# Loading the operands of RWKV's inverses in two halves, scaling its output later, and loading three attention units first

## The chip, the cores and the metric

The kernel runs on one core of one Trainium2 chip. The metric is device time in microseconds from launch to the last output. Its engines are TensorE (PE; its weight loads are listed apart as PEld), VectorE (DVE), ScalarE (ACT), GpSimd (POOL) and SyncE (SP), which here only issues DMAs. Every engine works through its own instructions in the order in which the program holds them; an instruction that waits holds up all behind it on its engine.

## The reference

One layer over 2048 tokens of width 1024. `x` is normalised and projected by `w_in`; the columns go to two branches whose outputs, 512 wide each, are joined, projected by `w_out` and added to `x`, with a last norm.

```python
def rwkv7_scan(r, decay, k, v, kk, a):       # 8 heads of 64
    def step(S, inp):
        r_t, w_t, k_t, v_t, kk_t, a_t = inp
        sa = jnp.einsum('bhij,bhj->bhi', S, -kk_t)
        S = (S * w_t[:, :, None, :]
             + sa[..., None] * (kk_t * a_t)[:, :, None, :]
             + v_t[..., None] * k_t[:, :, None, :])
        return S, jnp.einsum('bhij,bhj->bhi', S, r_t)
...
    y = (y - mu) * lax.rsqrt(var + GN_EPS) * gn_g + gn_b      # per head
    y = y + jnp.sum(r * k * r_k, axis=-1, keepdims=True) * v
    return y * jax.nn.silu(gate)

def attend(args):                             # blocks of 128 queries, 8 heads
    logits = jnp.einsum('bqhd,bsd->bqhs', qi, k_idx)          # index scores
    score = jnp.einsum('bqh,bqhs->bqs', wi, jax.nn.relu(logits))
    _, idx = lax.top_k(jnp.where(causal[None], score, -jnp.inf), topk)   # 256 keys
    s = jnp.einsum('bqhr,bqkr->bhqk', qa, c_sel)
    p = jax.nn.softmax(jnp.where(valid[:, None], s, -jnp.inf), axis=-1)
    return jnp.einsum('bhqk,bqkr->bqhr', p, c_sel)
```

## The kernel before

Four phases are written one after the other: `phase_as` (projections, and for every block of queries a mask of the 256 chosen keys, all stored in DRAM), `phase_r` (RWKV), `phase_t` (attention) and `phase_w` (the output projection). A scheduler turns them into one order for each engine. It takes the instruction of the best priority that its own timing says is ready; `e.later(n)` makes priorities worse by n steps, so attention (`later(2)`) and the output (`later(3)`) fill what RWKV leaves, and `tc.issue_after(x)` keeps an instruction behind x. Tiles of one tag share a fixed number of buffers (the last argument of `tl`), and a new tile of that tag waits until the old one has been read.

RWKV is not run token by token. The 2048 tokens are 16 batches n of 128, each of two halves (`chain(..., n, 0)` and `chain(..., n, 1)`) of 64 tokens, and all 8 heads are done at once; two units i = 0, 1 hold four heads each. A batch goes through these steps:

- `prep(n, i)`: loads `ld` (five quantities in one DMA), forms the scaled keys `BK` and queries `X` on DVE (eight operations, lines 950 to 967), and multiplies them on PE into `E`, which DVE copies under a mask (line 977).
- `systems`: `E` holds triangular blocks of 32 x 32, and `dma` carries them to DRAM (`du`, 4 DMAs) and back as `A`, where each of 32 systems stands in four partitions (the source is read four times).
- `inverse`: POOL inverts all of them at once in 31 iterations of two instructions (`Xtmp`, line 1031, and `Xr`, line 1033). The result goes to DRAM (`dx`) and back as `TT` (4 DMAs).
- `chain`: PE solves with `TT` (line 1068) and updates the state `S` (DVE, line 1096), one half batch after the other.
- `tail_norm` and `tail_out`: the norm of the batch's output `y`. DVE forms sums (`gst`), POOL raises them to -1/2 (line 1112), DVE scales `y` (line 1113); PE transposes `y` (line 1120), ACT writes `yo` (line 1126), POOL adds and multiplies (lines 1128, 1129), and SP stores it (line 1130) with the loads of `gr` (line 1124) beside it.

At step n of the loop the kernel runs `inverse` of batch n+1, the norm of batch n-1 behind it, `prep` of batch n+2, and `chain` of batch n. `A` and `Xr` have one buffer each.

Attention has 64 units, p = 0 to 3 (two heads each) by b = 0 to 15 (blocks of 128 queries); unit (p, b) has b+1 key blocks of 128. For every key block PE forms the scores (lines 1261 and 1262), DVE adds the mask (line 1263), ACT takes the exponential, PE transposes the weights of the two heads (line 1295, two transposes a key block), ACT copies them and PE multiplies with the values (line 1304). `load` fetches a unit's keys, queries, mask and gate one unit ahead. The output projection of a block of 128 tokens has 48 matmuls (lines 1381, 1382 and 1384) and needs both branches' results for it; its weights are loaded once RWKV's memory is free.

Of the kernel before, what the change touches and what calls it, by code (L numbers as in the profile page):

```python
# [7 lines left out]
F32 = mybir.dt.float32  # L8
# [6 lines left out]
OP = mybir.AluOpType  # L15
# [3 lines left out]
T = 2048  # L19
# [867 lines left out]
def phase_r(env):  # L887


    e = NS(env)  # L890
# [4 lines left out]
    W = 2 * C  # L895
# [112 lines left out]
    def systems(us):  # L1008

        du = e.dram([2, 2, NU, 32, 32], F32, nm("du"))  # L1010
        A = tl([128, 32, 32], F32, "A")
        for i, u in enumerate(us):
            for k in range(2):
                ps_ = slice(64 * i + k * 32, 64 * i + k * 32 + 32)
                dma(du[i, k].rearrange("u s t -> s u t"),
                    u.E[ps_, :, :, k * 32:k * 32 + 32].rearrange("s h c t -> s (h c) t"))
        dma(A.rearrange("l s t -> l (s t)"),
            du.rearrange("i k u s t -> (i k u) (s t)")[None].to_broadcast([4, 32, 1024]))
        return A

    def inverse(A):

        dx = e.dram([2, 2, NU, 32, 32], F32, nm("dx"))
        Xr = tl([128, 8, 32], F32, "Xr")
        G.memset(Xr, 0.0)
        for j in range(4):
            G.memset(Xr.rearrange("p i t -> p (i t)")[32 * j:32 * j + 32, j:256:36], 1.0)
        tmp = tl([128, 8, 32], F32, "Xtmp")
        for s in range(31):
            m, w = s // 4 + 1, 31 - s  # L1030
            G.tensor_tensor(tmp[:, :m, :w], Xr[:, :m, s:s + 1].to_broadcast([128, m, w]),  # L1031
                            A[:, s:s + 1, s + 1:].to_broadcast([128, m, w]), op=OP.mult)
            m_ = G.tensor_tensor(Xr[:, :m, s + 1:], Xr[:, :m, s + 1:], tmp[:, :m, :w], op=OP.add)  # L1033
        dma(dx.rearrange("i k u (r j) t -> j (i k u) r t", j=4), Xr)
        TT = tl([128, NU, 32], F32, "TT", 2)
        for i in range(2):
            for k in range(2):
                dma(TT[Q[2 * i + k]], dx[i, k].rearrange("u s t -> s u t"))
        return TT, m_.ins
# [60 lines left out]
    def tail_norm(y):  # L1100

        yv = y.rearrange("t c (h i) -> t (c h) i", h=2)
        st = tl([128, 3, NU], F32, "gst", 2)
        V.tensor_reduce(st[:, 0], yv, axis=AX.X, op=OP.add)
        V.tensor_scalar(st[:, 0], st[:, 0], 1.0 / 64, None, op0=OP.mult)
        bc = lambda a: a[:, :, None].to_broadcast([128, NU, 64])
        V.tensor_tensor(yv, yv, bc(st[:, 0]), op=OP.subtract)
        sq = tl([128, NU, 64], F32, "ysq")
        S.activation(sq, yv, AF.Square)
        V.tensor_reduce(st[:, 1], sq, axis=AX.X, op=OP.add)  # L1110
        V.tensor_scalar(st[:, 1], st[:, 1], 1.0 / 64, 64e-5, op0=OP.mult, op1=OP.add)
        m = G.tensor_tensor(st[:, 2], st[:, 1], e.mhalf[:, :NU], op=OP.pow)  # L1112
        V.tensor_tensor(yv, yv, bc(st[:, 2]), op=OP.mult)
        return m.ins

    def tail_out(us, y):

        pt = pst([128, NC, 2, C], "ch", 1)
        for c in range(NC):
            PE.transpose(pt[:, c].rearrange("p a b -> p (a b)"), y[:, c], ident)  # L1120
        for i, u in enumerate(us):
            yo = tl([128, 2, W], F32, "yo", 2)
            gr = tl([128, 2, W], F32, "gr", 2)
            dma(gr, e.d_gr4.rearrange("p (g i) t -> p g i t", i=2)[:, :, u.i, u.sl])
            for g, p in enumerate(u.ps):
                S.activation(yo[:, g].rearrange("p (a b) -> p a b", a=2), pt[:, 2 * g:2 * g + 2, i], AF.Identity,
                             scale=e.gng[:, p:p + 1], bias=e.gnb[:, p:p + 1])
            G.tensor_tensor(yo, yo, u.bv, op=OP.add)
            G.tensor_tensor(yo, yo, gr, op=OP.mult)  # L1129
            dma(e.d_y.rearrange("p (g i) t -> p g i t", i=2)[:, 0:2, u.i, u.sl], yo)  # L1130
# [28 lines left out]
    for n in range(N):  # L1159
# [3 lines left out]
        with e.later():  # L1163
            if nx:
                nx.TT, first = inverse(nx.A)
            if b0:
                with behind(first):
                    tail_norm(y0)
            if new:
                with behind(state):  # L1170
                    new.us.append(prep(n + 2, 0, new.eC, first))
        y = tl([128, NC, 128], F32, "y", 2)
        state = chain(b.us, b.TT, b.eC, y, n, 0)
        with e.later():
            if nx:
                for u in nx.us:
                    prep2(u)
# [7 lines left out]
                tail_out(b0.us, y0)  # L1185
        y0, b0 = y, b
    with e.later():
        tail_norm(y0)
        tail_out(b0.us, y0)


def phase_t(env):
# [11 lines left out]
        return ps.tile(shape, F32, name=nm(tag), tag=tag, bufs=bufs)  # L1204


    sel0 = tl([4, 256], F32, "sel0").rearrange("p (c a b) -> p c a b", c=2, a=2)
    V.memset(sel0, 1.0)
    G.affine_select(sel0, sel0, pattern=[[2, 2], [1, 2], [0, 64]], base=0, channel_multiplier=-1,
                    compare_op=OP.is_equal, fill=0.0)  # L1210
# [108 lines left out]

    units = [(p, b) for p in range(NP) for b in range(NB)]  # L1320
    last, stores, marks = None, [], {}
    load(*units[0])
    for i, u in enumerate(units + [None]):
        out = []
        ready, stores = stores, []
        if i + 1 < len(units):
            with tc.issue_after(load(*units[i + 1])):
                for x in ready:
                    dma(*x)
# [90 lines left out]
```

## Time and profile before

| | |
|---|---|
| three runs | 2094.41, 2101.48 (median), 2104.39 us |
| the profiled execution | 2104.7 us, span 2102.9 us |
| PE busy | 1803.3 us (86%) |
| PE weight loads busy | 1421.8 us (68%) |
| DVE busy | 1296.7 us (62%) |
| ACT busy | 1019.8 us (48%) |
| POOL busy | 795.3 us (38%) |
| mean granted clock of PE | 0.906 |
| DMA over the span | 126 GB/s |

The span runs from the first instruction to the last. Busy shares are means over phases with different limits: the projections end at about 980 us, RWKV with attention in its gaps follows to about 1760 us, and the rest of attention with the output projection makes the end. Idle time of an engine counts only where something late waits for that engine.

### The profile page before, as it was taken

Reading aid. Unit: us, or ns where it says so; the run is one execution under the profiler, and the core shown is the slowest. Engines: PE = TensorE matmul, PEld = TensorE weight load, DVE = VectorE, ACT = ScalarE, POOL = GpSimd, SP = SyncE. Lnnn points to the kernel's source line nnn. Section 1 sums busy time; section 2 is a strip of 40 time slices with the busy share of each in tenths; the row PEclk is TensorE's granted clock in tenths of the full one; section 3 lists DMA queues with packets and bytes.
Section 4 is the critical chain, followed back from the end, with each engine's and each line's share of the span. In section 5 each row is a group of like instructions: output and inputs, shape, how many; then the busy total and the mean of one; then the engine's idle time right before and its main releaser. Section 6 shows DMA issues by size and latency. Waiting matters only on the chain.

```text
span 2102.9 us, 36153 instructions
## 1 busy us (share of the span) xinstructions
PE 1803.3 (86%) x12906; PEld 1421.8 (68%) x12906; DVE 1296.7 (62%) x3050; ACT 1019.8 (48%) x1966; POOL 795.3 (38%) x1925
## 2 busy tenths in 40 slices
PE   5788998879796988986788988886988889899998
PEld 4666877658575867765566766665766667587776
DVE  5532538979779698986656557564756654644432
ACT  4422494453444744441355555454655567643431
POOL 1110124353544354562445645654546650100000
PEclk9778999989798999998799998798988899999999
DMA  7526334332262434234844355343454324744223
GB/s 248 199 94 200 108 101 135 101 115 85 75 239 63 135 107 136 91 95 125 204 102 105 95 136 147 105 119 98 115 143 131 93 78 108 233 128 128 66 93 112
DMA packets 309038, 262.50 MB, mean 125 GB/s; under 512 B 82544, under 2 KB 258288, under 8 KB 307696
## 3 DMA queue, kind: packets, MB, share of 16 engines
q1 hardware_dynamic: 304464, 248.03, 40.1%
q0 software_dynamic: 4384, 12.06, 1.8%
q8 instruction: 104, 1.70, 0.4%
q14 instruction: 86, 0.70, 0.1%
HBM read 166.37 MB, written 97.85 MB: 126 GB/s over the span
## 4 chain that ended last, share of the span: by engine, by line
PE 23%; POOL 14%; DMA 12%; issue 5%; DVE 4%; SPq 1%; ACT 1%; POOLq 0%; DVEq 0%; ACTq 0%
DMA A<-du 6%; POOL Xr L1033 6%; POOL Xtmp L1031 5%; PE om L1304 3%; PE po L1381 3%; PE po L1382 3%; PE po L1384 3%; PE tr L1295 3%; DMA dx<-Xr 2%; PE s L1261 2%; PE s L1262 1%; DMA TT<-dx 1%; DMA ld<-d_rw 1%; POOL yo L1129 1%; POOL gst L1112 1%
## 5 line engine op out<-in xcount | busy, mean ns | idle before, releaser
L577 PE MATMUL pm<-xh,wh 128*128 128x512 f32 x800 | 330.4, 414 | 20.3 <-DVE t L588 11.8
L578 PE MATMUL pm<-xl,wh 128*128 128x512 f32 x800 | 327.0, 409 | 0.0
L579 PE MATMUL pm<-xh,wl 128*128 128x512 f32 x800 | 326.1, 408 | 0.0
L1263 DVE CUSTOM_DVE_ANT_0 sc<-s,mk 128x512 f32<-128x512 f32 (+3 forms) x320 | 187.9, 607 | 102.8 <-PE s L1262 76.0
L1297 ACT ACTIVATE pt<-tr 128x512 f32<-128x512 f32 (+1 forms) x288 | 157.9, 569 | 160.8 <-PE tr L1295 115.9
L1031 POOL TENSOR_TENSOR Xtmp<-Xr,A 128x60 f32<-128x60 f32 (+24 forms) x496 | 146.9, 296 | 225.8 <-DMA A<-du 181.8
L577 PEld LDWEIGHTS pm<-xh,wh 128*128 128x128 f32 x800 | 158.1, 198 | 61.7 <-DVE t L588 13.7
L1270 ACT ACTIVATE sc<-sc,mx 128x128 f32<-128x128 f32 (+15 forms) x128 | 153.0, 1198 | 63.0 <-DVE mx L1269 62.7
L1295 PE MATMUL tr<-ident,sc 128*128 128x128 f32 x1088 | 180.1, 292 | 3.0 <-ACT pt L1297 2.6
L579 PEld LDWEIGHTS pm<-xh,wl 128*128 128x128 f32 x800 | 157.3, 197 | 36.4
L578 PEld LDWEIGHTS pm<-xl,wh 128*128 128x128 f32 x800 | 158.0, 197 | 35.4
L1304 PE MATMUL om<-pt,vt 128*64 128x128 f32 x2176 | 174.0, 295 | 6.2 <-DVE ga L1287 6.2
L1261 PE MATMUL s<-kt,q 128*128 128x512 f32 (+2 forms) x320 | 144.2, 454 | 35.8 <-DVE mx L1263 32.2
L1033 POOL TENSOR_TENSOR Xr<-Xr,Xtmp 128x60 f32<-128x60 f32 (+24 forms) x496 | 151.3, 305 | 37.4
L1304 PEld LDWEIGHTS om<-pt,vt 128*64 128x64 f32 x2176 | 134.2, 146 | 37.6 <-issue 19.6
L1295 PEld LDWEIGHTS tr<-ident,sc 128*128 128x128 f32 x1088 | 133.5, 149 | 33.9 <-issue 11.4
L317 ACT ACTIVATE mk<-x,st 128x1920 bf16<-128x1920 f16 (+5 forms) x72 | 98.0, 1361 | 103.6 <-POOL st L314 103.6
L249 ACT ACTIVATE rl<-lg,wi 128x512 f32<-128x512 f32 (+3 forms) x152 | 94.0, 631 | 99.6 <-PE lg L247 53.1
L1262 PE MATMUL s<-kt,q 128*128 128x512 f32 (+2 forms) x320 | 123.3, 389 | 8.1 <-DMA q<-d_q 8.0
L320 DVE TENSOR_SCALAR_CACHE_REDUCE mk<-x,st 128x2048 bf16<-128x2048 f16 (+5 forms) x72 | 120.6, 1675 | 1.4
L254 DVE SCALAR_TENSOR_TENSOR xs<-rl,wi,xs 128x512 f32<-128x512 f32 (+3 forms) x108 | 73.5, 681 | 60.9 <-ACT rl L249 60.1
L1387 POOL TENSOR_TENSOR st<-st 128x1 f32<-128x1 f32 x16 | 3.1, 195 | 277.1 <-ACT po L1386 277.1
(329 smaller groups left out, 3937.7 us busy)
## 6 DMA issues: line engine op xcount, KB each, us to landing
wraw<-in_w_in_dram SPq DMA_DIRECT2D x42, 512.0 KB
d_rw<-t SPq DMA_DIRECT2D x80, 256.0 KB
ld<-d_rw SPq DMA_DIRECT2D x32, 640.0 KB
q<-d_q SPq DMA_DIRECT2D x128, 128.0 KB
d_q<-t SPq DMA_DIRECT2D x32, 256.0 KB
d_kt<-t SPq DMA_DIRECT2D x32, 256.0 KB
kt<-d_kt SPq DMA_DIRECT2D x32, 256.0 KB
A<-du SPq DMA_DIRECT2D x16, 512.0 KB
```

Of the source, the lines that this page charges most:

```text
L577: PE.matmul(pm, wh[:, k], XH[g][:, k], start=k == 0, stop=False)
L578: PE.matmul(pm, wh[:, k], XL[g][:, k], start=False, stop=False)
L579: PE.matmul(pm, wl[:, k], XH[g][:, k], start=False, stop=k == KD - 1)
L1031: G.tensor_tensor(tmp[:, :m, :w], Xr[:, :m, s:s + 1].to_broadcast([128, m, w]), A[:, s:s + 1, s + 1:].to_broadcast([128, m, w]), op=OP.mult)
L1033: m_ = G.tensor_tensor(Xr[:, :m, s + 1:], Xr[:, :m, s + 1:], tmp[:, :m, :w], op=OP.add)
L1261: PE.matmul(pS[:, :wp], qh[:, h, qs], k[:, h, :wp], start=True, stop=False)
L1262: PE.matmul(pS[:, :wp], ql[:, h, qs], k[:, h, :wp], start=False, stop=True)
L1263: V.tensor_tensor_reduce(out=rows[h][:, c0:c0 + w], in0=pS[:, :w], in1=mk[:, c0:c0 + w], scale=1.0, scalar=LOW, op0=OP.add, op1=OP.max, ac ...
L1270: marks[p, b] = S.activation(rows[h][:, :n], rows[h][:, :n], AF.Exp, bias=mx[:, h, 4:5], accum_out=sums[:, h:h + 1]).ins
L1295: PE.transpose(pt[:, i, h], rows[h][:, (kb + i) * 128:(kb + i) * 128 + 128], ident)
L1297: S.activation(w[:, :m], pt[:, :m], AF.Copy)
L1304: PE.matmul(po[HALF[h]], v[:, (kb + i) % 4, HALF[h]], w[:, i, h], start=kb + i == 0, stop=kb + i == b)
```

## The change

The operands of the inverses lie in two tiles: `A`, rows 0 to 15 of every system, with two buffers, and `A2`, rows 16 to 31, with one. Each has its own DMA of 256 KB, and `inverse` reads from the one that holds row s. `tail_norm` returns the scaling as a function, and the loop calls it after the first half of `chain`, behind that half's state update, where it used to stand ahead of it; after the loop it is called at once. `yo` has one buffer instead of two. `sel0` no longer has a tile of its own: it uses one of the four score buffers `sc`. The first three units' loads are issued at a priority three steps better, ahead of RWKV's own, and the loop loads from the fourth on.

```diff
     def systems(us):
 
         du = e.dram([2, 2, NU, 32, 32], F32, nm("du"))
-        A = tl([128, 32, 32], F32, "A")
+        A = tl([128, 16, 32], F32, "A", 2), tl([128, 16, 32], F32, "A2")
         for i, u in enumerate(us):
             for k in range(2):
                 ps_ = slice(64 * i + k * 32, 64 * i + k * 32 + 32)
                 dma(du[i, k].rearrange("u s t -> s u t"),
                     u.E[ps_, :, :, k * 32:k * 32 + 32].rearrange("s h c t -> s (h c) t"))
-        dma(A.rearrange("l s t -> l (s t)"),
-            du.rearrange("i k u s t -> (i k u) (s t)")[None].to_broadcast([4, 32, 1024]))
+        rows = du.rearrange("i k u s t -> (i k u) (s t)")
+        for j in range(2):
+            dma(A[j].rearrange("l s t -> l (s t)"), rows[None, :, j * 512:j * 512 + 512].to_broadcast([4, 32, 512]))
         return A
@@
         for s in range(31):
             m, w = s // 4 + 1, 31 - s
+            row = A[0][:, s:s + 1, s + 1:] if s < 16 else A[1][:, s - 16:s - 15, s + 1:]
             G.tensor_tensor(tmp[:, :m, :w], Xr[:, :m, s:s + 1].to_broadcast([128, m, w]),
-                            A[:, s:s + 1, s + 1:].to_broadcast([128, m, w]), op=OP.mult)
+                            row.to_broadcast([128, m, w]), op=OP.mult)
@@
-        m = G.tensor_tensor(st[:, 2], st[:, 1], e.mhalf[:, :NU], op=OP.pow)
-        V.tensor_tensor(yv, yv, bc(st[:, 2]), op=OP.mult)
-        return m.ins
+        rpow(st[:, 2], st[:, 1])
+        return lambda: V.tensor_tensor(yv, yv, bc(st[:, 2]), op=OP.mult)
@@
-            yo = tl([128, 2, W], F32, "yo", 2)
+            yo = tl([128, 2, W], F32, "yo")
@@
             if b0:
                 with behind(first):
-                    tail_norm(y0)
+                    scale = tail_norm(y0)
...
         state = chain(b.us, b.TT, b.eC, y, n, 0)
         with e.later():
+            if b0:
+                with behind(state):
+                    scale()
             if nx:
                 for u in nx.us:
                     prep2(u)
@@
-        tail_norm(y0)
+        tail_norm(y0)()
         tail_out(b0.us, y0)
@@
-    sel0 = tl([4, 256], F32, "sel0").rearrange("p (c a b) -> p c a b", c=2, a=2)
+    sel0 = tl([128, T], F32, "sc", 4)[0:4, 0:256].rearrange("p (c a b) -> p c a b", c=2, a=2)
@@
-    load(*units[0])
+    with e.later(-3):
+        for u in units[:3]:
+            load(*u)
     for i, u in enumerate(units + [None]):
         out = []
         ready, stores = stores, []
-        if i + 1 < len(units):
+        if 3 <= i + 1 < len(units):
```

The scheduler makes new orders from this, and all of RWKV, attention and output stands a little differently. On SP, a step of the loop where the result of one inverse (`dx`, `TT`) and the operands of the next (`du`, `A`) follow each other, before:

```order
L1034 DMA dx_1459_8400<-Xr_1460_8401 4x256x32
L1015 DMA du_1501_8668<-E_1496_8648 32x8x32 x2
L937 DMA ld_1545_8998<-d_rw_63 128x10x128
L1038 DMA TT_1462_8471<-dx_1459_8400 32x8x32 x4
L1017 DMA A_1502_8669<-du_1501_8668 128x1x1024
L1232 DMA q0_2520_14754<-d_q0_66 64x2x256 x2
```

and the same step now:

```order
L1036 DMA dx_1462_8406<-Xr_1463_8407 4x256x32
L1015 DMA du_1504_8674<-E_1499_8654 32x8x32 x2
L1335 DMA d_y_93<-ga_2423_14339 128x128
L1040 DMA TT_1465_8477<-dx_1462_8406 32x8x32 x4
L1019 DMA A_1505_8675<-du_1504_8674 128x1x512
L1019 DMA A2_1506_8676<-du_1504_8674 128x1x512
L937 DMA ld_1549_9006<-d_rw_63 128x10x128
```

Both halves stand where the one load stood, behind `dx` and `TT` of the inverse before; `ld` has moved behind them. On DVE, the scaling of batch 6's `y` (line 1113) and the second `E` of batch 9 (line 977), before:

```order
L964 TENSOR_TENSOR BK_10858<-ld_10848,L_10852 128x4x64
L979 SCALAR_TENSOR_TENSOR ld_10848<-ld_10848,rkc 128x128 x2
L1269 TENSOR_REDUCE mx_15960<-mx_15960 128x1 x2
L977 TENSOR_TENSOR E_10868<-rp_10869,mask_7751 128x512
L977 TENSOR_TENSOR E_10868<-rp_10870,mask_7751 128x512
L1287 TENSOR_TENSOR ga_15756<-ga_15756,om_15974 128x128
L1263 ISA sc_16073,mx_16075<-s_16077,mk_15953 128x512
L1263 ISA mx_16075 128x1
L1263 ISA sc_16074,mx_16075<-s_16081,mk_15953 128x512
L1263 ISA mx_16075 128x1
L1278 RECIPROCAL sums_15961<-sums_15961 128x2
L1113 TENSOR_TENSOR y_10376<-y_10376,gst_10696 128x512
```

and now, where it is line 1115:

```order
L1098 TENSOR_TENSOR S_1345_7771<-ch_10812,SP_10779 64x4x64 x2
L1115 TENSOR_TENSOR y_10391<-y_10391,gst_10714 128x512
L950 SCALAR_TENSOR_TENSOR L_10870<-restart_7748,ld_10866 128x256
L959 TENSOR_TENSOR BK_10876<-ld_10866 128x4x64
L962 TENSOR_SCALAR ka_10878<-ld_10866,kac,oka 128x128 x2
L1321 TENSOR_TENSOR ga_16102<-ga_16102,om_16375 128x128
L1082 TENSOR_TENSOR SP_10930<-S_1345_7771,eC_9893 64x256 x2
L1267 ISA sc_16476,mx_16477<-s_16501,mk_16340 128x512
```

The scaling stood behind `E`; now it follows the state update `S` and comes ahead of the whole preparation, whose `E` stands 22 rows further down. On SP again, the place of the last inverse's result, before:

```order
L1242 DMA mk_3370_17986<-d_mask15_86 128x2048
L1329 DMA d_y_93<-ga_3249_17503 128x128
L1034 DMA dx_2173_13209<-Xr_2174_13210 4x256x32
L1244 DMA ga_3407_18133<-d_ga_62 128x128
L1038 DMA TT_2176_13280<-dx_2173_13209 32x8x32 x4
L1232 DMA q0_3404_18125<-d_q0_66 64x2x256 x2
L1232 DMA q1_3405_18128<-d_q1_67 64x2x256 x2
L1242 DMA mk_3406_18131<-d_mask0_71 128x128
```

and now:

```order
L1246 DMA mk_3646_18981<-d_mask10_81 128x1408
L1036 DMA dx_2189_13241<-Xr_2190_13242 4x256x32
L1040 DMA TT_2192_13312<-dx_2189_13241 32x8x32 x4
L1335 DMA d_y_93<-ga_3535_18579 128x128
L1248 DMA ga_3647_18983<-d_ga_62 128x128
L1335 DMA d_y_93<-ga_3555_18648 128x128
L1248 DMA ga_3673_19083<-d_ga_62 128x128
L1246 DMA mk_3672_19081<-d_mask11_82 128x1536
```

The next mask to be loaded was that of block 0 of the last p; now it is that of its block 11. Attention stands ten to eleven units further on at this point of RWKV.

## Rows read from the trace of the kernel before

**Rows 1.** Stretches: us, busy of PE, PEld, DVE, ACT, POOL, clock, DMA share, GB/s.

```profile
1101.30:1758.80 657.50, 557.60 (x6390) 433.47 (x6389) 385.48 (x1183) 365.80 (x829) 361.00 (x1030) 0.89 0.43 112
1758.80:2103.00 344.20, 323.64 (x2183) 256.59 (x2182) 144.68 (x363) 149.36 (x304) 22.77 (x57) 0.97 0.41 128
```

**Rows 2.** Waits: engine, line, releaser, us in total, times, longest.

```profile
POOL Xtmp L1031 <- DMA A<-du: 181.8, 14, 18.6
...
DVE y L1113 <- POOL gst L1112: 74.0, 11, 15.6
```

**Rows 3.** SP's issues in one step of RWKV: start, us, what.

```profile
1177.88 0.58 SPq L1034 DMA_DIRECT2D dx<-Xr  x1
1182.59 1.81 SPq L1038 DMA_DIRECT2D TT<-dx  x4
...
1186.94 0.57 SPq L1017 DMA_DIRECT2D A<-du  x1
```

**Rows 4.** POOL's timeline: first product of seven of the inverses.

```profile
1152.10 0.24 POOL L1031 TENSOR_TENSOR Xtmp<-Xr,A 128x31 f32<-128x31 f32 x1 [11.86 <-DMA A<-du]
...
1197.78 0.24 POOL L1031 TENSOR_TENSOR Xtmp<-Xr,A 128x31 f32<-128x31 f32 x1 [14.19 <-DMA A<-du]
...
1250.71 0.24 POOL L1031 TENSOR_TENSOR Xtmp<-Xr,A 128x31 f32<-128x31 f32 x1 [16.65 <-DMA A<-du]
...
1426.84 0.24 POOL L1031 TENSOR_TENSOR Xtmp<-Xr,A 128x31 f32<-128x31 f32 x1 [13.11 <-DMA A<-du]
...
1477.18 0.28 POOL L1031 TENSOR_TENSOR Xtmp<-Xr,A 128x31 f32<-128x31 f32 x1 [12.54 <-DMA A<-du]
...
1531.54 0.24 POOL L1031 TENSOR_TENSOR Xtmp<-Xr,A 128x31 f32<-128x31 f32 x1 [17.18 <-DMA A<-du]
...
1705.71 0.24 POOL L1031 TENSOR_TENSOR Xtmp<-Xr,A 128x31 f32<-128x31 f32 x1 [12.69 <-DMA A<-du]
```

**Rows 5.** The chain of waits through one long step: start, us, what.

```profile
1223.79 1.62 POOL gst L1112
...
1232.80 1.28 DVE E L977 x2
...
1237.71 12.94 DMA A<-du
```

**Rows 6.** SP's issue of the last load of `A`.

```profile
1695.69 0.55 SPq L1017 DMA_DIRECT2D A<-du  x1
```

**Rows 7.** Busy time while that load flows.

```profile
1697.00:1704.60 7.60, 7.60 (x72) 5.77 (x70) 6.14 (x18) 7.27 (x15) 0.00 (x0) 1.00 0.27 76
```

**Rows 8.** The chain of waits: a store of 64 KB of attention.

```profile
1585.72 1.94 DMA d_y<-ga
```

**Rows 9.** SP's issues at the start of RWKV.

```profile
981.01 0.58 SPq L937 DMA_DIRECT2D ld<-d_rw  x1
...
997.12 2.53 SPq L1232 DMA_DIRECT2D q<-d_q  x4
...
1055.67 0.57 SPq L1034 DMA_DIRECT2D dx<-Xr  x1
...
1066.39 1.81 SPq L1038 DMA_DIRECT2D TT<-dx  x4
```

**Rows 10.** Attention's transposes up to 1758.8 us and behind it: count, busy, mean ns.

```profile
L1295 PE MATMUL tr<-ident,sc 128*128 128x128 f32 x758 | 130.0, 299 | 2.0 <-ACT pt L1297 1.7 <-ACT sc L1270 0.4
...
L1295 PE MATMUL tr<-ident,sc 128*128 128x128 f32 x330 | 50.1, 278 | 1.0 <-ACT pt L1297 0.9
```

**Rows 11.** PE's groups between 1850 and 2050 us: count, busy, mean ns.

```profile
L1382 PE MATMUL po<-wl,yh 128*128 128x512 f32 x175 | 69.9, 399 | 0.0
...
L1295 PE MATMUL tr<-ident,sc 128*128 128x128 f32 x200 | 29.5, 275 | 0.0
```

**Rows 12.** PE's timeline in the output projection.

```profile
2047.03 1.98 PE L1384 MATMUL po<-wh,yl 128*128 128x512 f32 x8
...
2052.47 1.98 PE L1384 MATMUL po<-wh,yl 128*128 128x512 f32 x8
```

## The prediction

> **What bounds the kernel now.** Read the page first, then the stretches, then one step of the loop. The change leaves the first half of the program as it is: the two programs stand in the same order on every engine up to about 980 us, where the projections end. After that attention fills the gaps of RWKV, and I cut the rest at the first matmul on the second inverse's result (1101.3 us) and on the last one's (1758.8 us). Between them PE is busy 557.6 of 657.5 us at a mean granted clock of 0.89 of full speed (a mixture of its two levels, 1.2 and 2.4 GHz); behind them it is busy 323.6 of 344.2 us at 0.97 [rows 1]. So the last stretch is bound by PE, and the RWKV stretch, with 99.9 us of PE idle, by something else.
>
> What that is, the waits say: POOL stands 181.8 us in 14 waits for `A`, and DVE 74.0 us in 11 waits for POOL's power `gst` [rows 2]. One step shows a ring with no slack: POOL ends an inverse, SP issues `dx` at 1177.88, its landing lets SP issue `TT` at 1182.59, then `du`, then `A` at 1186.94 [rows 3], and POOL starts the next inverse at 1197.78 [rows 4]. Thirteen inverses start between 1152.10 and 1705.71 [rows 4]: 12 steps of 46.1 us, about 26 of them the inverse itself (1197.78 to the power at 1223.79 [rows 4, 5]).
>
> The steps are not alike. Where DVE's scaling `y` by `gst` stands ahead of the work that makes `E` for the coming `A`, the ring is longer: the inverse ends, `gst` runs at 1223.79, `E` only follows at 1232.80, `A` at 1237.71 [rows 5]. DVE's order has this in three of the 12 steps (the starts at 1250.71, 1477.18 and 1531.54), with two to eight of the eight operations of that preparation behind the scaling, and they took 52.9, 50.3 and 54.4 us, mean 52.5 [rows 4]. Where the scaling stands just ahead of `E`, with none of those operations behind it (three steps), a step took 45.7 (1152.10 to 1197.78). All nine that are not of the first kind share the rest, 553.6 - 157.6 = 396.0, mean 44.0.
>
> **The change part by part**, against the profiled execution's own 2104.7 us (span 2102.9), 3.2 above the median of the three runs, 2101.48.
>
> *The double buffer.* It could let `A` be loaded during the inverse before it. SP's order takes that back: from the third inverse on, `A` and `A2` still stand behind `dx` and `TT` of the inverse before, and SP issues in order, so no load of them can start before that inverse has ended and `dx` has landed. Only the second inverse has its `A` ahead of `dx`. What remains is the size: POOL starts on half the bytes. A load with nothing beside it took 1695.69 to 1705.71, 10.0 us [rows 4, 6]; between 1697.0 and 1704.6 the DMA engines were busy at a share of 0.27, 4.3 of 16 [rows 7]. Bounds for 256 KB: 10.0 (no gain), and 4.7, what `dx` with 128 KB took [rows 3]. I take half of the 7.6 us of flow away, 3.8, near the middle. The rest lands about 4 us later, while 16 of the 31 iterations at 0.84 us (26.0 / 31) come first: hidden. The second issue costs SP 0.57 more a step [rows 3]; what stands behind it, `ld` of the step after next, can wait. Over 12 steps -45.6, and -7.6 for the third and fourth inverse.
>
> The Trainium skill ("DMA: Bandwidth & Descriptors", section "Rules for kernel authors") says that a leading broadcast of c copies confines a DMA to at most c engines; `A` is read as four copies. The share of 0.27 agrees. By the rule each half flows for half the time on the same four engines, which is the 3.8; if a half were instead spread wider, the first would land near the lower bound and the gain would be up to 5.3 a step, 64 over twelve.
>
> *The scaling, half a step later.* In DVE's order it now stands directly or soon behind the state update of the first half of a step, and that is ahead of `E` in all 12 steps: in seven with five or more of the eight operations behind it, in five with at most one. The wait for `gst` is not gone, then; it moves from behind `E` to ahead of it. At the prices above: 7 x 52.5 + 5 x 45.7 = 596.0 instead of 553.6, +42.4. With the halves the loop gains 10.8 in all. Bounds: 12 x 44.0 if DVE always comes after the power (-25.6 before the halves), 12 x 52.5 (+76.4).
>
> *One `yo`.* ACT's second pair now waits for the store of the first. In POOL's order four to six iterations lie between the two uses, 3.4 to 5 us; the store takes between 1.9 (a `ga` of 64 KB [rows 8]) and 4.7 (`dx`), and ACT's two activations and issue about 1.5. So POOL waits 0 to 2.8 a step; I take 1.0, 14 for 14 steps. Two buffers hid this.
>
> *Three units first.* Their 17 loads take SP some 10 us (four `q` took 2.53, 0.63 each [rows 9]), so `ld`, issued at 981.01, goes about 10 later. Against that, `dx` of the first inverse, issued at 1055.67, landed only at 1066.39 behind the load of the second `A` [rows 9], 10.7 instead of 4.7, and that `A` is now there early: 13 us at most, with the wait for it. PE gets attention where it had none. I take 0 for the second inverse's result (-10 to +10).
>
> *What moves between stretches.* This is the large term. PE's order has 758 of the 1088 transposes of attention ahead of the first matmul on the last `TT`, as the trace has (758 and 330 [rows 10]); now it has 904. So 73 key blocks (two transposes each) leave the last stretch. Their price: between 1850 and 2050 us PE was full; the output's three lines have 525 matmuls there (175 + 174 + 176) and 100 blocks [rows 11]; 24 matmuls take 5.44 us (2047.03 to 2052.47 [rows 12]), so 525 take 119.0, which leaves 81.0, 0.81 a block. 73 x 0.81 = 59.1 off a stretch that PE bounds. In the RWKV stretch they must fit into 99.9 of idle; it would then be as dense as the last one (40.8 of 657 is 6%, 20.6 of 344 also 6%). Bounds 0 and 59; I take a quarter, +15.
>
> Sum: 0 - 10.8 + 14 + 15 - 59.1 = -40.9: 2064. The power itself is the same operation at the same place in POOL's order. `sel0` borrows one of the four score buffers before the first scores, where PE waits for loads anyway; if that cover goes, it costs the first unit the few operations that build `sel`, once, and the bounds of the start hold it.
>
> **The rivals.**
>
> *The wait for A really goes.* If the ring fell well below PE's work, PE would bound both stretches: 557.6 x 0.89 / 0.97 + 59.1 = 571, at 6% idle 607, 50 less than now, and the 59 from the end: 1995. For it: 181.8 us of wait. Against: SP's order, and `gst` ahead of `E`. Chance 0.11.
>
> *The scaling stops DVE.* On the other side: the wait for `gst` comes right behind the state update, before attention's scores, which have two buffers; so PE stops with DVE. If all 12 waits were as long as the longest now, 15.6, they would be 187, 113 more than the 74.0; 41 find PE idle, 72 do not: 2064 + 72 - 15 (the crowding is then in it) = 2121. It decides from about 14 us a wait (74 + 41 + 55 over 12). For it: the place in the order. Against: PE has more attention ahead of each state update, so DVE comes to it later. Chance 0.14.
>
> *One yo stops ACT.* ACT reaches the second pair before POOL has begun the inverse in which the first is added, and the copies behind it wait. At 3 us a step on PE's path, over the POOL's 1, 13 steps cost 39: 2103, no change. For it: one to nine instructions between the pairs; against: ACT is busy only 365.8 of the 657.5 us [rows 1]. Chance 0.15.
>
> **How the numbers follow.** The forecast has 0.60, own range 2035 to 2092. A measurement here can tell about 0.5%, 10.5 us: faster means under 2091. Faster: 0.57 of the forecast, 0.11, 0.01 of the yo case: 0.69. Same: 0.03 and 0.14: 0.17. Slower: 0.14. For 8 in 10 the range reaches from 2008, which leaves most of the first rival out, to 2112.
>
> **What would show it.** Right: the loads of `A` behind `TT` in time; the first product of an inverse about 6 us after the issue of `A`, POOL's waits for it near 130; steps of 43 to 48 us; the last `TT` within 25 us of now and some 285 us from its first matmul to the end; 904 transposes ahead of it. Wrong: `A` in place when an inverse starts; DVE's waits for `gst` far over 74, with PE idle beside them; ACT waiting for `d_y` stores; or a last stretch that keeps its 344 us because the output's weights come too late.

## The result, and the profile after

The changed kernel took 2069.81 us (median of 4 runs, 2063.44 to 2073.18) against 2097.94 us of the kernel before beside it (4 runs, 2093.71 to 2104.39): a ratio of 0.9854, 95% interval 0.9822 to 0.9886. It is faster by 1.5%; the forecast was 2064. The profiled execution took 2069.04 us with a span of 2067.3.

The same two stretches as before [rows 1], cut at the first matmul on the second and on the last `TT` (us, busy time and count of PE, PEld, DVE, ACT and POOL, granted clock of PE, DMA share, GB/s):

```profile
1101.90:1792.90 691.00, 605.04 (x6840) 472.81 (x6839) 405.81 (x1307) 399.86 (x918) 354.80 (x1030) 0.90 0.48 120
1792.90:2067.30 274.40, 259.79 (x1654) 209.39 (x1653) 110.60 (x214) 104.92 (x199) 22.40 (x57) 0.98 0.38 125
```

The start has not moved (1101.9 against 1101.3). The RWKV stretch is 33.5 us longer than before (691.0 against 657.5), the last one 69.8 shorter (274.4 against 344.2). Attention's transposes, first up to 1792.9 us and then behind it, show why the end is shorter; before it was 758 and 330 [rows 10]:

```profile
L1299 PE MATMUL tr<-ident,sc 128*128 128x128 f32 x904 | 147.8, 293 | 2.6 <-ACT pt L1301 1.4 <-ACT sc L1274 1.1
...
L1299 PE MATMUL tr<-ident,sc 128*128 128x128 f32 x185 | 27.0, 277 | 1.1 <-ACT pt L1301 1.1
```

Of the 73 key blocks that left the end, 61 now stand in the RWKV stretch (791 transposes between 1101.9 and 1792.9 us, 668 in the stretch before) and 12 ahead of it.

Why the RWKV stretch is longer is seen in its waits (engine, line, releaser, us in total, times, longest). [rows 2] counts the whole run; within the RWKV stretch before, POOL waited 163.2 us for `A`, and DVE the same 74.0 us for the power:

```profile
POOL Xtmp L1033 <- DMA A<-du: 147.3, 14, 13.8
ACT yo L1127 <- DMA d_y<-yo: 66.9, 10, 10.8
...
PE ch L1053 <- ACT yo L1127: 57.3, 12, 8.4
DVE gst L1112 <- ACT ysq L1111: 45.8, 10, 8.6
...
DVE y L1115 <- POOL gst L130: 6.6, 2, 5.2
```

DVE's wait for the power is as good as gone (6.6 us, it was 74.0). New ones have come: ACT waits for the store of `yo`, and both PE and DVE wait for ACT. DVE's stands at the sums of the norm, which need the squares that ACT forms (line 1111); it was 2.6 us in the stretch before. One step shows how they hang together. First what ACT and PE did there (start, us, what, and in brackets the idle time before it with its releaser), then the chain of waits:

```profile
1358.13 0.81 ACT L1127 ACTIVATE yo<-ch,gnb,gng 128x128 f32<-128x128 f32 x2 [9.49 <-DMA d_y<-yo]
...
1358.99 1.12 PE L1053 MATMUL ch<-S,X 128*64 128x128 f32 x8 [7.65 <-ACT yo L1127]
```

```profile
1354.54 0.68 POOL yo L1129
1355.48 0.68 POOL yo L1130
1356.19 1.83 DMA d_y<-yo
1358.13 0.82 ACT yo L1127 x2
1358.99 1.12 PE ch L1053 x8
...
1386.97 1.27 DVE E L977 x2
1388.63 1.68 DMA du<-E
1390.36 6.89 DMA A<-du
```

ACT has written the first unit's `yo` and wants to write the second. There is one buffer, so the first must be stored; POOL adds and multiplies it only between iterations of an inverse, at 1354.54. ACT stands 9.49 us. The transposed `y`, which it still has to read, lies in the PSUM tile of the tag `ch`, which has one buffer too and which `chain` uses for its own products, so PE's next `chain` (line 1053) stands 7.65 us behind ACT. From it the chain runs on to `E`, `du` and `A`: the late `E` makes the step long.

The loads of `A` behaved as forecast. They are issued behind `dx` and `TT` (start, us, what):

```profile
1373.60 0.58 SPq L1036 DMA_DIRECT2D dx<-Xr  x1
1378.33 1.80 SPq L1040 DMA_DIRECT2D TT<-dx  x4
1390.36 1.15 SPq L1019 DMA_DIRECT2D A<-du  x2
...
1740.08 1.14 SPq L1019 DMA_DIRECT2D A<-du  x2
```

and the first product of three of the inverses, among them the one behind the load at 1390.36 and the last one, follows at

```profile
1142.87 0.24 POOL L1033 TENSOR_TENSOR Xtmp<-Xr,A 128x31 f32<-128x31 f32 x1 [7.36 <-DMA A<-du]
...
1397.32 0.27 POOL L1033 TENSOR_TENSOR Xtmp<-Xr,A 128x31 f32<-128x31 f32 x1 [9.09 <-DMA A<-du]
...
1746.42 0.24 POOL L1033 TENSOR_TENSOR Xtmp<-Xr,A 128x31 f32<-128x31 f32 x1 [8.57 <-DMA A<-du]
```

1740.08 to 1746.42 is 6.3 us from issue to use, where [rows 4, 6] have 10.0; over the 12 steps the mean fell from 12.1 to 7.6. From 1142.87 to 1746.42 there are 12 steps of 50.3 us, against 46.1 before. So a step became 4.5 us shorter at the load and 8.7 longer elsewhere.

### The profile page after: what moved, and what is told of

The parts are those of the page before. It is cut to its first block, busy times and chain, and to the rows that moved or that the text cites. A ratio compares the mean times of both kernels' runs of the same rounds, so it can differ in the third digit from the quotient of the medians.

```text
span 2067.3 us, 36192 instructions
## 1 busy us (share of the span) xinstructions
PE 1792.3 (87%) x12906; PEld 1417.0 (69%) x12906; DVE 1287.3 (62%) x3050; ACT 1017.7 (49%) x1966; POOL 788.4 (38%) x1925
## 4 chain that ended last, share of the span: by engine, by line
PE 28%; DMA 11%; POOL 9%; DVE 4%; issue 3%; ACT 2%; SPq 1%; POOLq 0%; ACTq 0%; DVEq 0%
DMA A<-du 5%; PE om L1308 4%; PE tr L1299 3%; POOL Xtmp L1033 3%; POOL Xr L1035 3%; PE po L1387 3%; PE po L1388 3%; PE po L1390 3%; PE s L1265 2%; PE s L1266 2%; DMA dx<-Xr 1%; PE ch L1070 1%; DMA d_y<-yo 1%; DMA du<-E 1%; PE rp L974 1%
## 5 line engine op out<-in xcount | busy, mean ns | idle before, releaser
L1033 POOL TENSOR_TENSOR Xtmp<-Xr,A 128x60 f32<-128x60 f32 (+24 forms) x496 | 145.0, 292 | 199.1 <-DMA A<-du 163.5
L1299 PE MATMUL tr<-ident,sc 128*128 128x128 f32 x1088 | 174.5, 290 | 3.7 <-ACT pt L1301 2.6
L1308 PEld LDWEIGHTS om<-pt,vt 128*64 128x64 f32 x2176 | 132.8, 145 | 52.3 <-DVE ga L1291 27.3
L1387 PE MATMUL po<-wh,yh 128*128 128x512 f32 x256 | 101.0, 395 | 1.2 <-ACT yh L1378 1.2
```

Source lines behind the costliest of these rows:

```text
L1299: PE.transpose(pt[:, i, h], rows[h][:, (kb + i) * 128:(kb + i) * 128 + 128], ident)
L1308: PE.matmul(po[HALF[h]], v[:, (kb + i) % 4, HALF[h]], w[:, i, h], start=kb + i == 0, stop=kb + i == b)
L1387: PE.matmul(po, yh[:, m], wh[:, m, ds], start=m == 0, stop=False)
```

## The experiments

Theory 1, formed from these rows: one `yo` costs time on the chip, through ACT and PE, and the halves give it back; what is left of the gain is the attention that now stands ahead of the last `TT`. Theory 2: with more attention in it the RWKV stretch is bound by PE's work, and the waits are only where its idle time shows. All ratios below are against the kernel before in runs on the same chip. All stretches are cut as above.

### One `yo` alone

```diff
-            yo = tl([128, 2, W], F32, "yo", 2)
+            yo = tl([128, 2, W], F32, "yo")
```

> The kernel before with one change alone: `yo` in one buffer. Its program already has 904 transposes ahead of the last `TT`, as the changed kernel has (before: 758). Theory 1 (the waits for the single buffer are on the path: some 4 us a step, which the smaller loads of `A` give back): end stretch 274 us, RWKV stretch 691 + 12 x 4.5 = 745, in all 1101 + 745 + 274 + 2 = 2122 us, slower than before by 1%. Theory 2 (with more attention in it the RWKV stretch is bound by PE's work, and the waits are only the place where its idle time shows): 691 and 274 as in the changed kernel, 2068 us; one buffer would then be the whole gain.

Measured: 2109.52 us, ratio 1.0048 (1.0031 to 1.0066).

```profile
1100.30:1838.00 737.70, 619.91 (x6917) 481.13 (x6917) 415.77 (x1333) 408.04 (x934) 347.94 (x1030) 0.89 0.45 113
1838.00:2110.80 272.80, 258.19 (x1654) 208.26 (x1653) 109.92 (x213) 104.89 (x199) 22.43 (x57) 0.99 0.38 126
```

```profile
ACT yo L1126 <- DMA d_y<-yo: 111.7, 14, 13.3
...
PE ch L1051 <- ACT yo L1126: 71.6, 13, 11.2
```

This one edit brings both: the last stretch falls by 71.4 us to that of the changed kernel, and the RWKV stretch grows by 80.2. The scheduler, which knows that the second pair must wait for the store, puts attention into the time; on the chip the stretch grows by more than the end gives back. Theory 2 is out as it stood: the buffer is not the gain, it is a small loss. The 2122 of theory 1 was 12 too many.

### Two `yo` again

```diff
-        A = tl([128, 16, 32], F32, "A", 2), tl([128, 16, 32], F32, "A2")
+        A = tl([128, 16, 32], F32, "A"), tl([128, 16, 32], F32, "A2")
...
-            yo = tl([128, 2, W], F32, "yo")
+            yo = tl([128, 2, W], F32, "yo", 2)
```

> The changed kernel with two buffers for `yo` again and one for each half of `A` (so that it fits). 816 transposes stand ahead of the last `TT`, 44 key blocks fewer than in the changed kernel: end stretch 274 + 44 x 0.81 = 310 us. Theory 1: ACT's wait for the store (66.9 us) and PE's for ACT (57.3 us) go, steps of 46 instead of 50.3, RWKV stretch 638, in all 2052 us. Theory 2: the stretch is shorter by the moved blocks alone, 655, in all 2069 us, no change against the changed kernel.

Measured: 2049.16 us, ratio 0.9758 (0.9738 to 0.9777).

```profile
1104.80:1727.10 622.30, 558.96 (x6507) 434.35 (x6506) 394.48 (x1192) 371.14 (x842) 367.50 (x1030) 0.91 0.48 124
1727.10:2048.70 321.60, 304.57 (x1988) 240.02 (x1986) 135.65 (x329) 136.40 (x275) 22.53 (x57) 0.98 0.40 126
```

Theory 1 (2052), though it had the shares a little differently: 622 and 322 instead of 638 and 310, with steps of 43.9 us instead of 46. The second buffer is worth 20.6 us, and no row of ACT waiting for `d_y` is left in the stretch.

### The halves alone

The diff of `systems` and `inverse` above, with one buffer for each half.

> The kernel before with `A` loaded in two halves alone, each half in one buffer. 758 transposes ahead of the last `TT`, so an end stretch of 344 us. Theory 1: some 4 us a step less, 13 steps, RWKV stretch 607, in all 2054 us. Theory 2 (the ring is not what sets the steps): 645 to 657, 2092 to 2104 us.

Measured: 2064.67 us, ratio 0.9832 (0.9808 to 0.9855).

```profile
1092.70:1710.60 617.90, 554.69 (x6437) 432.13 (x6437) 392.50 (x1190) 369.75 (x834) 367.17 (x1030) 0.92 0.47 121
1710.60:2059.80 349.20, 326.83 (x2183) 256.68 (x2182) 145.56 (x363) 150.49 (x304) 22.68 (x57) 0.97 0.40 127
```

The ring of inverse and load does set the steps: the stretch falls by 39.6 us with no less attention in it (678 transposes, 668 before), if not to the 607 of theory 1, and it starts 8.6 us earlier. This edit by itself is as fast as the changed kernel (0.9832 against 0.9854, the intervals overlap).

### Three units first alone

```diff
-    load(*units[0])
+    with e.later(-3):
+        for u in units[:3]:
+            load(*u)
...
-        if i + 1 < len(units):
+        if 3 <= i + 1 < len(units):
```

> The kernel before with the loads of three attention units ahead of RWKV's own alone. 796 transposes ahead of the last `TT`, 19 key blocks more than before: end stretch 344 - 15 = 329 us. If blocks fit into the idle time of the RWKV stretch: 2090 us; if each lengthens it by its price: 2104 us. The first matmul on the second `TT` within 10 us of 1101 us by both.

Measured: 2084.90 us, ratio 0.9930 (0.9908 to 0.9952).

```profile
1115.50:1758.20 642.70, 548.01 (x6370) 430.32 (x6371) 390.44 (x1169) 362.63 (x826) 359.96 (x1030) 0.90 0.46 116
1758.20:2086.20 328.00, 308.07 (x2057) 244.09 (x2056) 137.48 (x336) 139.53 (x283) 23.38 (x58) 0.98 0.40 127
```

RWKV starts 14.2 us later, past the 10 that both theories allowed, and yet its last `TT` comes when it did (1758.2 against 1758.8), with 19 key blocks more done. They are what the end gives back: 16.2 us, 0.85 each. 14.6 us of gain, the 2090 of the first case and a little more. But the blocks did not go where that case put them: ahead of 1115.5 us stand 130 transposes, 90 stood ahead of 1101.3, and the RWKV stretch holds 666 where it held 668. So this run says nothing of what a block costs in that stretch; why the stretch is 14.8 us shorter at the same attention is not shown.

### The order of one `yo`, without its wait

Two buffers, and an edge from the first store to the second pair that the scheduler times but the chip does not wait for. `A` has one buffer for each half.

```diff
-            yo = tl([128, 2, W], F32, "yo")
+            yo = tl([128, 2, W], F32, "yo", 2)
...
-                S.activation(yo[:, g].rearrange("p (a b) -> p a b", a=2), pt[:, 2 * g:2 * g + 2, i], AF.Identity,
-                             scale=e.gng[:, p:p + 1], bias=e.gnb[:, p:p + 1])
+                q = S.activation(yo[:, g].rearrange("p (a b) -> p a b", a=2), pt[:, 2 * g:2 * g + 2, i], AF.Identity,
+                             scale=e.gng[:, p:p + 1], bias=e.gnb[:, p:p + 1])
+                if i:
+                    tc.add_manual_dep(q.ins, out.ins.name, ORDER, reason="in the order of one yo")
...
-            dma(e.d_y.rearrange("p (g i) t -> p g i t", i=2)[:, 0:2, u.i, u.sl], yo)
+            out = dma(e.d_y.rearrange("p (g i) t -> p g i t", i=2)[:, 0:2, u.i, u.sl], yo)
```

> The changed kernel with two buffers for `yo` and one for each half of `A`, but with an edge that holds the second pair of `yo` behind the first store in the scheduler's timing only, so that the program's order stays close to the changed kernel's (880 transposes ahead of the last `TT`, it has 904), while ACT has nothing to wait for when it comes to the second pair. Theory 1 (the wait on the chip costs the time): ACT's wait for the store and PE's for ACT vanish, steps of about 46 us, RWKV stretch some 640, end stretch 274 + 12 x 0.81 = 284, in all 2028 us. Theory 2 (the order costs it: more attention stands inside each step of RWKV): steps of 50, 681 + 284, in all 2067 us.

Measured: 2041.22 us, ratio 0.9720 (0.9694 to 0.9746).

```profile
1107.70:1754.00 646.30, 578.34 (x6764) 451.83 (x6764) 412.54 (x1284) 391.65 (x901) 362.11 (x1030) 0.94 0.49 127
1754.00:2039.30 285.30, 269.27 (x1730) 215.96 (x1729) 117.29 (x238) 113.46 (x216) 22.49 (x57) 0.98 0.38 124
```

This tells the two causes apart best, since the order is nearly that of the changed kernel (880 against 904 transposes). Without the wait the steps are 46.6 us (theory 1: 46; theory 2: 50):

```profile
1149.87 0.24 POOL L1033 TENSOR_TENSOR Xtmp<-Xr,A 128x31 f32<-128x31 f32 x1 [8.24 <-DMA A<-du]
...
1709.25 0.24 POOL L1033 TENSOR_TENSOR Xtmp<-Xr,A 128x31 f32<-128x31 f32 x1 [8.88 <-DMA A<-du]
```

The stretch is 44.7 us shorter than the changed kernel's. 12 key blocks account for 9.7 of that; the other 35 are the wait's. The end is 10.9 longer, the start 5.8 later, so 28.0 us remain in the span, 28.6 in the medians. Theory 1's whole, 2028, was still 13 too low, by a start and a stretch that are each some 6 longer. No row of ACT waiting for a store stands in the stretch, PE's weight loads wait 1.1 us for `yo`, and DVE waits 3.6 us for the squares. And it beats two `yo` in their own order by 7.9 us, so attention that stands ahead is worth something as long as nobody stops for it: the 32 key blocks more lengthen the stretch by 24.0 us (0.75 each) and give 36.3 back at the end. Whether the 24.0 are the blocks' alone is not shown: in this order DVE has the scaling ahead of five or more of the eight operations that make `E` in nine of the 12 steps (47.6 us in the mean, the other three 43.7), with two `yo` in their own order in none. No run parts the two.

### The scaling alone

The edits of `tail_norm` and of the loop above, on the kernel before.

> The kernel before with the scaling half a step later alone. 730 transposes ahead of the last `TT`, 14 key blocks fewer than before: end stretch 355 us. My prediction's term (DVE reaches the scaling ahead of `E` in all steps and waits there for the power): RWKV stretch 657 + 42, in all 2157 us. Rival (DVE comes after the power, and the waits of 74 us go): RWKV stretch 632 to 645, 2090 to 2103 us.

Measured: 2108.01 us, ratio 1.0038 (1.0021 to 1.0055).

```profile
1100.60:1753.50 652.90, 549.01 (x6290) 425.40 (x6289) 381.05 (x1161) 357.38 (x817) 359.39 (x1030) 0.88 0.45 113
1753.50:2106.80 353.30, 334.44 (x2281) 263.66 (x2280) 150.79 (x385) 156.69 (x315) 22.85 (x58) 0.98 0.40 126
```

```profile
DVE y L1113 <- POOL gst L130: 80.8, 12, 12.4
```

Neither the 42 us nor the rival's 2090 to 2103 came, but the run does not test either, because this edit alone hardly moves the scaling in DVE's order. The wait for the power is as long as before (80.8 us), and the long steps are the same three (now 53.5, 52.1 and 57.5 us). They are again the ones in which the scaling stands ahead of operations that the coming `A` still needs (two, eight and five of the eight; before two, eight and four); the others took 37.0 to 47.0. In the first of the three, DVE does the scaling, one of the operations behind it and `E` here at

```profile
1224.78 1.52 DVE L1113 TENSOR_TENSOR y<-y,gst 128x512 f32<-128x512 f32 x1 [5.59 <-POOL gst L130]
...
1227.56 0.42 DVE L964 TENSOR_TENSOR BK<-ld,L 128x256 f32<-128x256 f32 x1
...
1232.22 1.29 DVE L977 TENSOR_TENSOR E<-rp,mask 128x512 f32<-128x512 f32 x2 [1.46 <-PE rp L974]
```

and in the kernel before it did the scaling at

```profile
1225.43 1.52 DVE L1113 TENSOR_TENSOR y<-y,gst 128x512 f32<-128x512 f32 x1 [5.60 <-POOL gst L1112]
```

The end, where 14 key blocks more are left, is 9.1 us longer, and the stretch only 4.6 shorter without them.

### One buffer for the first half of `A`

```diff
-        A = tl([128, 16, 32], F32, "A", 2), tl([128, 16, 32], F32, "A2")
+        A = tl([128, 16, 32], F32, "A"), tl([128, 16, 32], F32, "A2")
```

> The changed kernel with one buffer for the first half of `A` instead of two. Its program stands in the same order on every engine. If the second buffer does nothing, as the issues of `A` behind `TT` say: 2070 us, within 0.3% of the changed kernel. If loads used to start while an inverse still read the other buffer: a step longer by up to 4 us, 2118 us.

Measured: 2070.61 us (2066.79 to 2074.33), ratio 0.9855 (0.9820 to 0.9890), the changed kernel's 0.9854. The double buffer, the change's most visible edit, does nothing that can be measured.

### The load spread over partitions

On the kernel with two `yo`:

```diff
         for j in range(2):
-            dma(A[j].rearrange("l s t -> l (s t)"), rows[None, :, j * 512:j * 512 + 512].to_broadcast([4, 32, 512]))
+            for r in range(4):
+                dma(A[j].rearrange("l s t -> l (s t)")[32 * r:32 * r + 32], rows[:, j * 512:j * 512 + 512])
```

> The kernel with two `yo` (2049 us) with each half of `A` loaded by four DMAs of 32 partitions instead of one that reads its source four times. The program's order is otherwise the same. If the four copies confine a load to four DMA engines and the flow bounds it: the wait from issue to first product falls from some 7 to 5.5 us, 12 steps, 2031 us. If the fixed time of a DMA bounds it, three more issues of 0.57 us each stand ahead of the first half's end: 7 to 8.5 us, 2049 to 2067 us.

Measured: 2004.39 us, ratio 0.9543 (0.9516 to 0.9570), the fastest of all.

```profile
1101.70:1694.30 592.60, 552.34 (x6507) 429.13 (x6506) 396.54 (x1192) 369.98 (x842) 371.46 (x1030) 0.93 0.50 130
1694.30:2013.40 319.10, 302.34 (x1988) 239.95 (x1986) 135.52 (x329) 135.58 (x275) 22.53 (x57) 0.98 0.40 127
```

POOL's waits for `A` in the stretch:

```profile
POOL Xtmp L1034 <- DMA A<-du: 94.1, 13, 13.2
```

SP's issues of the last load and POOL's first product on it, in the timeline:

```profile
1636.74 3.78 SPq L1020 DMA_DIRECT2D A<-du  x8
...
1640.29 0.24 POOL L1034 TENSOR_TENSOR Xtmp<-Xr,A 128x31 f32<-128x31 f32 x1 [6.91 <-DMA A<-du]
```

The busy time while it flows (columns as in the stretches):

```profile
1637.20:1640.20 3.00, 3.00 (x30) 1.99 (x26) 0.81 (x4) 2.44 (x6) 0.00 (x0) 1.00 0.57 173
```

3.6 us from issue to use, where the broadcast half of the changed kernel took 6.3, at a DMA share of 0.57. The whole broadcast load had 0.27 [rows 7], the broadcast halves 0.37, with other transfers beside them:

```profile
1741.00:1746.00 5.00, 5.00 (x42) 3.87 (x41) 4.45 (x17) 3.10 (x6) 0.00 (x0) 1.00 0.37 117
```

The gain is 45 us by the medians, more than twice the 18 expected. The profiled execution, 11 us above its median, shows 35 of them: the stretch is 29.7 us shorter, and POOL's waits for `A` in it fell from 128.9 to 94.1 us.

### The same on the kernel before, and nothing else

```diff
-        dma(A.rearrange("l s t -> l (s t)"),
-            du.rearrange("i k u s t -> (i k u) (s t)")[None].to_broadcast([4, 32, 1024]))
+        for r in range(4):
+            dma(A.rearrange("l s t -> l (s t)")[32 * r:32 * r + 32], du.rearrange("i k u s t -> (i k u) (s t)"))
```

> The kernel before with the one load of `A` (512 KB) cut by partitions into four DMAs of 32 partitions, and nothing else. 716 transposes ahead of the last `TT`, 21 key blocks fewer: end stretch 361 us. If the source's four copies confined the load to few DMA engines: issue to first product falls from 12 to some 6 us, steps of 40 to 41, RWKV stretch 585, in all 2050 us. If the fixed time of a DMA or the bytes bound it: 10 to 12 us as before, 2100 to 2120 us.

Measured: 2035.25 us, ratio 0.9700 (0.9671 to 0.9729): twice the gain of the whole change, from one line. In the timeline SP issues the last load, and POOL uses it, at

```profile
1615.67 1.71 SPq L1018 DMA_DIRECT2D A<-du  x4
...
1620.69 0.24 POOL L1031 TENSOR_TENSOR Xtmp<-Xr,A 128x31 f32<-128x31 f32 x1 [7.63 <-DMA A<-du]
```

and while it flows, the engines are busy as follows (columns as in the stretches):

```profile
1616.50:1620.60 4.10, 3.70 (x42) 2.87 (x41) 1.90 (x9) 4.10 (x11) 0.00 (x0) 1.00 0.66 193
```

The same 512 KB take 5.0 us instead of 10.0 [rows 4, 6], the DMA engines being busy at 0.66 instead of 0.27 [rows 7]; over the 12 steps the mean from issue to use is 6.4 us instead of 12.1. That is the first case; its 2050 was 15 too high, as RWKV also starts 14.3 us earlier (1087.0 us). The rule cited in the prediction (the Trainium skill, "DMA: Bandwidth & Descriptors", section "Rules for kernel authors": a leading broadcast of c copies confines a DMA to at most c engines) fits from the other side: without the broadcast the share passes 4 of 16. The edit also makes four DMAs out of one, and no run parts the two.

### Four DMAs with the order of one `yo`, without the late scaling, and without halves

Three combinations of the edits above.

> The kernel with two `yo` in the order of one (2041 us) with each half of `A` loaded by four DMAs of 32 partitions. 880 transposes stand ahead of the last `TT`. If the ring of inverse and loads still sets the steps, the 45 us that the four DMAs brought to the kernel with two `yo` come here too: steps of 43 us, 1996 us. If PE's work bounds the RWKV stretch by now, with 32 key blocks more in it than there: stretch 593 + 32 x 0.81 = 619 and 285 behind it, 2007 us or more, no better than the kernel with two `yo` and four DMAs (2004 us).

> The kernel with two `yo` and four DMAs for each half of `A` (2004 us), with the scaling back at its old place ahead of the first half of the chain. 816 transposes ahead of the last `TT`, as there. If the place of the scaling is worth nothing: 2004 us, within 0.5%. If waits for the power ahead of `E` cost as they did in three of the twelve steps of the kernel before (8.5 us each): 2025 to 2035 us. If the later place costs: 1990 us.

> The kernel before with the load of `A` in four DMAs of 32 partitions and the first three attention units loaded ahead of RWKV; `A` in one tile, two `yo`, the scaling at its old place. 816 transposes ahead of the last `TT`, as in the kernel with halves and four DMAs each (2004 us). If the halves are worth something once the load is spread over the partitions (512 KB instead of 256 KB ahead of the first product): 2035 - 15 = 2020 us. If the spread load was all: 2004 us, within 0.5%.

Measured: four DMAs a half in the order of one `yo`, 2007.71 us, ratio 0.9561 (0.9534 to 0.9588); four DMAs a half with the scaling at its old place, 2004.82, ratio 0.9552 (0.9524 to 0.9580); four DMAs for the whole of `A` with three units first, 2017.23, ratio 0.9595 (0.9571 to 0.9619).

```profile
1100.60:1720.50 619.90, 573.75 (x6762) 445.92 (x6761) 413.44 (x1284) 391.62 (x901) 365.64 (x1030) 0.95 0.51 132
1720.50:2008.60 288.10, 272.61 (x1730) 218.70 (x1729) 116.77 (x238) 113.63 (x216) 22.49 (x57) 0.97 0.38 123
```

The rows are those of the first. With the short loads PE is busy 573.8 of 619.9 us, and 32 key blocks more lengthen this stretch by 27.3 (0.85 each) while the end gives 31.0: no gain is left in putting attention ahead, the second case of what was expected. The edit of the scaling changes nothing (2004.82 against 2004.39), but here too DVE has the scaling at the same place with it and without it, so what the place is worth is not tested. The halves still bring some 11 us once the load is spread (ratios 0.9543 and 0.9595, whose intervals just miss each other; the medians, 2004.39 and 2017.23, differ by 13).

## Why the prediction was right, and where it was not

The time was 6 us from the forecast because errors cancelled. In the RWKV stretch the forecast was 15.3 too low, at the end 10.7 too high, and it started from an execution of 2104.7 us where the median before became 2097.94: 40.9 less was forecast, 35.7 measured between the profiled executions and 28.1 between the medians. Of its own signs of being right, steps of 43 to 48 us (50.3) and a last `TT` within 25 us (34.1 later) did not come; of its signs of being wrong, ACT waiting for `d_y` did. By the prediction's own steps, with single edits as the yardstick (medians against before: halves -34.8, three units -14.6, one `yo` +10.0, scaling +8.6; sum -30.8, the whole change -28.1):

- **Start, 0 forecast**: right in the changed kernel (+0.6), though three units alone move it by 14.2 and the halves by -8.6.
- **Halves of A, -3.8 a step**: right in kind and close in size. The load alone went from 10.0 to 6.3 us (6.2 forecast), the mean over the steps fell by 4.5, and the double buffer is undone by SP's order, as the kernel with one buffer shows. POOL's total wait was 163.5 us in the whole run instead of near 130, with `E` later.
- **Scaling ahead of `E` in all 12 steps, +42.4**: the place came as forecast, the price is open. In the changed kernel seven steps have five or more of the operations behind the scaling (51.9 us in the mean) and five at most one (48.1), but DVE comes to the scaling after the power (6.6 us of wait in all), because the state update ahead of it comes late, from a `chain` that waited. The forecast had DVE wait for the power there; it waits for ACT instead (45.8 us). The two runs on this edit alone, one of them with four DMAs, have the scaling nearly at the same place in DVE's order with it and without it, so they show neither that the term is nothing nor that it is 42. In the kernel before, and with the edit alone, the steps with operations behind the scaling are the long ones, as the prediction read it. That rival's 2121, in which DVE stands for the power, is out.
- **One `yo`, +14**: this is the step that failed: mis-sized, and put at the wrong engine. I had POOL wait for 1.0 us a step. It is ACT that waits (66.9 us) and PE behind it (57.3), the mechanism of the third rival; at nearly the same order it is worth 28.6 us in the whole and 35 in the stretch. I had not seen that the transposed `y` shares its only PSUM buffer with `chain`, which carries ACT's wait to PE. The rival's 39 on top of the 14 was too much against 28.6, so its 2103 did not come. With 35 of the stretch's 33.5 for the wait, -1.5 is left for halves, scaling and crowding together, where +4.2 was forecast.
- **Crowding of PE, +15, a quarter of the price**: of the 73 blocks 61 went into the stretch and 12 ahead of it. What 61 cost there no run shows by itself; 32 more came with 0.75 each in the order of one `yo`, the place of the scaling included. If that is the blocks' price, a quarter was too little.
- **RWKV stretch in all, +18.2 forecast**: +33.5. Single edits sum to +21.2 (halves -39.6, three units -14.8, scaling -4.6, one `yo` +80.2); the other 12.3 come from their meeting and stay unexplained.
- **73 key blocks off the end, -59.1**: the count was right (904 and 185 transposes), the price too low: -69.8, 0.96 each; one `yo` alone, with the same 73, gave 0.98, three units first 0.85. Which edit moved them I had not asked: it is mostly the single `yo`, alone enough for all 904.

That the wait for `A` would really go was a rival for this change. Its 1995 was nearly reached, 2004, by another edit, so the argument that the ring sets the steps was right, and a shorter load made the ring shorter where a second buffer did not.

## What to carry to other kernels

Before a second buffer is given to a load, look at what its issue stands behind; if it is late anyway, make the load itself shorter, here by cutting it along the partitions instead of broadcasting the source. A buffer taken from another tile to pay for it has two prices that must be looked at apart: the order that the scheduler makes of it, and the waits on the chip, which reach as far as the other resources that the waiting instruction holds (here one PSUM tile). When several edits come together, run each alone: here one of them was worth as much as all, and taking another one back gained 20 us. And see first whether an edit run alone moves what it is meant to move: the scaling's did not, and a time that stays the same then says nothing of it.

## What the runs showed of the hardware that was not expected

PE's granted clock is part of the gain and was in no term of the sum. In the RWKV stretch it was 0.89 before, 0.90 after, 0.94 without the wait for `yo` and 0.95 with the short loads in the order of one `yo`. Between the changed kernel and the one without the wait PE's busy time fell from 605.0 to 578.3 us, of which 12 key blocks explain 9.7; the other 17 go with the clock. PE's pauses behind ACT (57.3 us, none without the wait) may have lowered it, but they are not the whole of it: with two `yo` in their own order PE waits 1.1 us for ACT's `yo`, and the clock is 0.91. What sets it was not tried.

Cutting a load into four DMAs adds issues on SP (3.78 us for eight, 1.15 for two), and these cost nothing that shows: the first product on four DMAs came 3.6 us after the first issue.
